# Attention on one core: the scores, too, in 2x2 blocks with Strassen's seven products

## Chip, cores, metric

One core of one Trainium2 chip. The metric is the device time of one execution in microseconds (us).

## The reference

Inputs q, k and v are float32, 8 x 2048 x 512. The result has the same shape.

```python
scores = np.matmul(q, k.transpose(0, 2, 1)) / np.sqrt(512)
attn_weights = special.softmax(scores, axis=-1).astype(np.float32)
return np.matmul(attn_weights, v)
```

## The kernel before

A query tile has 512 queries, so there are 32 tiles (4 in each of 8 batches). Scores are kept transposed: 128 keys on the partitions, 512 queries along the columns. Matmuls are in fp16 and sum in fp32 in tiles of PSUM; the kernel uses eight such tiles of 512 fp32 columns, called banks here. The output product (exponentials times v) is already computed in 2x2 blocks with the seven products of Strassen's method in Winograd's form; the scores are computed plainly. While the output products of tile g run, the scores of tile g + 1 are put between them.

```python
ps_st = ... tile_pool(name="ps_st", bufs=3, space=PSUM)    # scores
ps_x  = ... bufs=2;   ps_y = ... bufs=1;   ps_z = ... bufs=2   # outputs: 5 banks
# ... cut
def qk_tile(g, kb):                      # 128 keys x 512 queries
    # ... cut
    for dc in range(ND):                 # ND = 4
        nc.tensor.matmul(st[:], kT[b, c][:, n, dc, :], qT[b, qt][:, :, dc, :],
                         start=(dc == 0), stop=(dc == ND - 1))
    nc.scalar.activation(out=pt[:, kb // 2, kb % 2, :], in_=st[:], func=EXP, scale=inv_sqrt_d)

def p_sums(g, j0, j1):                   # sums of exponentials for the output products
    # ... cut
    nc.vector.tensor_add(s1[:, js], a21, a22)
    nc.vector.tensor_sub(a21, a11, a21)
    nc.vector.tensor_sub(s2[:, js], s1[:, js], a11)
    nc.vector.tensor_sub(s4[:, js], a12, s2[:, js])

class Pair:                              # two output blocks; pairs "a" and "b" in each tile
    def product(self, n):
        # ... cut: eight 128x256 matmuls into bank x, y or z
        getattr(self, f"after{n}", lambda: None)()
    def scaled(self, tag, src, r):       # VectorE
        t = small.tile([P, H], F32, tag=tag)
        nc.vector.tensor_scalar_mul(out=t[:], in0=src, scalar1=r[:])
        return t
    def after5(self):
        nc.vector.reciprocal(out=self.r2[:], in_=self.z[:, H:H + 1])   # r2: cut
        self.p5 = self.scaled("p5", self.z[:, 0:H], self.r2)
    # ... cut: after3, after2, after6, after7, after4

ORDER = "a1 a5 b5 a3 b1 a2 a6 b3 a7 b2 b6 a4 b7 b4".split()
# ... cut
p_sums(0, NJ - GROUP, NJ)                # end of the prologue
dma_transpose("q", 0, 1)                 # the second query tile
```

The softmax here doesn't subtract the row's maximum and nothing guards it: scores larger than these inputs give would overflow.

## Time and profile before

| | |
|---|---|
| time | 871.78 us (median of 3 runs, 871.65 to 871.78) |
| TensorE (PE) / VectorE (DVE) / ScalarE (ACT) busy | 97% / 55% / 35% |
| one score tile, one output product | 0.87 us each |

The first fence is from the page of the kernel before: its span, busy time by engine, granted clock in 40 slices, and the chain of waits that ended last by engine and by line.

```profile
span 870.3 us, 13872 instructions
...
PE 846.7 (97%) x5712; PEld 557.3 (64%) x5712; DVE 475.1 (55%) x1162; ACT 307.0 (35%) x513; POOL 72.7 (8%) x116
...
PEclk9799999999999999999999999999999999999999
...
PE 95%; DMA 4%; DVE 0%; issue 0%; POOL 0%; ACT 0%; POOLq 0%
```

After the prologue TensorE works almost without a pause, and the chain of waits stays on it. The next fence is the timeline of TensorE in the middle of the kernel before. The columns are start, length of the merged piece, engine, line, operation, and what is written from what. A piece's length (1.03 us) runs past the start of the next piece (0.87 us later), so rates are read from start to start.

```profile
453.13 1.03 PE L142 MATMUL st<-t 128*128 128x512 f16 x4
454.00 1.04 PE L193 MATMUL x<-t,pt 128*128 128x256 f16 x8
454.87 1.03 PE L142 MATMUL st<-t 128*128 128x512 f16 x4
```

Four matmuls of 512 columns take 0.87 us, and so do eight of 256 columns, each with its own weight load: 109 ns for one of 256. TensorE's waits in the whole execution (waits view: total us, times, longest) are few:

```profile
PE tr L100 <- DMA t<-in_q_dram: 9.5, 1, 9.5
PE st L142 <- DMA t<-t: 9.1, 1, 9.1
PE x L193 <- DVE o L206: 0.6, 1, 0.6
```

The first is the start. The second is in the prologue, where the second query tile waits for its DMA transpose.

### The profile page before, as it was taken

What the parts mean: (1) busy time and instruction counts of PE and PEld (TensorE: products, weight loads), DVE (VectorE), ACT (ScalarE), POOL (GpSimd) and SP (SyncE); (2) the same over time, 40 slices, a digit from 0 to 9 for tenths busy, and PEclk for the clock granted to TensorE, in tenths of its full rate; (3) what the DMA queues carried; (4) which work ended last, traced back from release to release, by engine and by line L of the source; (5) the groups of instructions that cost most, each with busy time, mean ns of one, the idle gap of its engine ahead of it and who ended that gap; (6) DMA issues with size and microseconds to landing.
All of it is one profiled execution on the core that took longest, in us unless ns stands there. A gap on an engine that the chain in (4) does not pass through costs nothing.

```text
span 870.3 us, 13872 instructions
## 1 busy us (share of the span) xinstructions
PE 846.7 (97%) x5712; PEld 557.3 (64%) x5712; DVE 475.1 (55%) x1162; ACT 307.0 (35%) x513; POOL 72.7 (8%) x116
## 2 busy tenths in 40 slices
PE   5599999999999999999999999999999999999997
PEld 3266666666666666666666666666666666666666
DVE  3554755556555574455654466555654557455554
ACT  2233333333333333333333333333333333333331
POOL 3111002010020100200002000110002010000000
PEclk9799999999999999999999999999999999999999
DMA  9999954986579954997439985298753988511101
GB/s 154 165 177 200 168 130 99 203 138 131 119 127 191 151 116 98 164 190 152 113 82 187 166 158 130 54 213 163 133 122 83 205 141 142 109 49 49 41 32 74
DMA packets 192046, 115.74 MB, mean 133 GB/s; under 512 B 126448, under 2 KB 175600, under 8 KB 191984
## 3 DMA queue, kind: packets, MB, share of 16 engines
q0 software_dynamic: 50688, 50.34, 38.3%
q1 hardware_dynamic: 141296, 64.54, 32.5%
q8 instruction: 44, 0.72, 0.3%
q14 instruction: 18, 0.15, 0.1%
HBM read 100.70 MB, written 33.55 MB: 154 GB/s over the span
## 4 chain that ended last, share of the span: by engine, by line
PE 95%; DMA 4%; DVE 0%; issue 0%; POOL 0%; ACT 0%; POOLq 0%
PE st L142 49%; PE x L193 26%; PE z L193 13%; PE y L193 6%; DMA t<-t 2%; DMA t<-in_q_dram 2%; PE tr L100 0%; POOL t L81 0%; ACT pt L146 0%; DVE o L206 0%; DVE t L202 0%; DVE o L239 0%; DVE s L155 0%; DVE pt L156 0%; DVE s L158 0%
## 5 line engine op out<-in xcount | busy, mean ns | idle before, releaser
L142 PE MATMUL st<-t 128*128 128x512 f16 x2048 | 514.9, 380 | 9.4 <-DMA t<-t 9.1
L146 ACT ACTIVATE pt<-st 128x512 f16<-128x512 f32 x512 | 305.7, 597 | 546.0 <-PE st L142 546.0
L142 PEld LDWEIGHTS <-t 128*128 128x128 f16 x2048 | 200.4, 98 | 159.1 <-DMA t<-t 9.6
L193 PEld LDWEIGHTS <-pt 128*128 128x128 f16 x2048 | 200.5, 98 | 81.5 <-issue 8.6
L193 PEld LDWEIGHTS <-s 128*128 128x128 f16 x1536 | 150.3, 98 | 58.2 <-issue 0.5
L193 PE MATMUL x<-vh,pt 128*128 128x256 f16 x1024 | 133.6, 274 | 0.0
L202 DVE TENSOR_SCALAR t<-x,r 128x256 f32<-128x256 f32 x128 | 61.9, 484 | 72.0 <-PE x L193 69.7
L155 DVE TENSOR_TENSOR s<-pt 128x512 f16<-128x512 f16 x128 | 53.5, 418 | 64.7 <-ACT pt L146 64.7
L193 PE MATMUL z<-vh,s 128*128 128x257 f16 x512 | 66.7, 273 | 0.4 <-DVE t L202 0.4
L193 PE MATMUL x<-t,pt 128*128 128x256 f16 x512 | 66.2, 272 | 0.6 <-DVE o L206 0.6
L193 PE MATMUL z<-t,s 128*128 128x257 f16 x512 | 66.6, 273 | 0.0
L193 PE MATMUL y<-vh,pt 128*128 128x256 f16 x512 | 66.4, 273 | 0.0
L193 PE MATMUL x<-t,s 128*128 128x256 f16 x512 | 66.4, 273 | 0.0
L239 DVE TENSOR_SCALAR o<-x,r 128x256 f32<-128x256 f32 x64 | 30.9, 483 | 58.7 <-PE x L193 58.7
L206 DVE SCALAR_TENSOR_TENSOR o<-y,r,t 128x256 f32<-128x256 f32 x64 | 30.9, 484 | 57.8 <-PE y L193 57.8
L156 DVE TENSOR_TENSOR pt<-pt 128x512 f16<-128x512 f16 x128 | 54.4, 425 | 4.4
L158 DVE TENSOR_TENSOR s<-pt,s 128x512 f16<-128x512 f16 x128 | 54.4, 425 | 4.4
L157 DVE TENSOR_TENSOR s<-s,pt 128x512 f16<-128x512 f16 x128 | 53.4, 417 | 0.0
L217 DVE RECIPROCAL r<-z 128x1 f32<-128x1 f32 x64 | 10.7, 167 | 67.3 <-PE z L193 67.3
L81 POOL DMA_DIRECT2D t<-in_k_dram x32 | 24.5, 767 | 200.7 <-DMA t<-t 192.6
L81 POOL DMA_DIRECT2D t<-in_q_dram x32 | 24.5, 766 | 188.6 <-DMA t<-t 134.5
L222 DVE RECIPROCAL r<-z 128x1 f32<-128x1 f32 x64 | 10.6, 165 | 43.6 <-PE z L193 43.6
(18 smaller groups left out, 183.6 us busy)
## 6 DMA issues: line engine op xcount, KB each, us to landing
out_dram<-o SPq DMA_DIRECT2D x128, 256.0 KB, 2.5
t<-in_k_dram POOLq DMA_DIRECT2D x32, 512.0 KB, 10.4
t<-in_q_dram POOLq DMA_DIRECT2D x32, 512.0 KB, 8.9
vh<-in_v_dram POOLq DMA_DIRECT2D x32, 512.0 KB, 10.9
t<-t SPq DMA_TRANSPOSE x59, 4.9
ident<-attn_identity SPq DMA_DIRECT2D x1, 32.0 KB, 1.6
```

What stands on the lines that cost most here:

```text
L81: nc.gpsimd.dma_start(out=t[:], in_=srcs[what][b, :, c * CH:(c + 1) * CH, :])
L142: nc.tensor.matmul(st[:], kT[b, c][:, n, dc, :], qT[b, qt][:, :, dc, :], start=(dc == 0), stop=(dc == ND - 1),)
L146: nc.scalar.activation(out=pt[:, kb // 2, kb % 2, :], in_=st[:], func=EXP, scale=inv_sqrt_d)
L155: nc.vector.tensor_add(s1[:, js], a21, a22)
L156: nc.vector.tensor_sub(a21, a11, a21)
L157: nc.vector.tensor_sub(s2[:, js], s1[:, js], a11)
L158: nc.vector.tensor_sub(s4[:, js], a12, s2[:, js])
L193: nc.tensor.matmul(dst[:, 0:width], lhs(j), rhs(j), start=(first and j == 0), stop=(j == NJ - 1), skip_group_check=True,)
L202: nc.vector.tensor_scalar_mul(out=t[:], in0=src, scalar1=r[:])
L206: nc.vector.scalar_tensor_tensor(out=out_, in0=src, scalar=r[:], in1=other[:], op0=MULT, op1=ADD)
L217: nc.vector.reciprocal(out=self.r2[:], in_=self.z[:, H:H + 1])
L239: nc.vector.tensor_scalar_mul(out=self.o2[:, 0:H], in0=self.x[:, 0:H], scalar1=self.r2[:])
```

## The change

Scores are computed for groups of 256 + 256 keys and 512 queries in 2x2 blocks with seven products instead of eight. That is worth one eighth of the score columns on TensorE. It costs additions: four VectorE operations for each block of keys and of queries, and seven reads of PSUM per group by ScalarE and VectorE in place of four (the exponentials of four key blocks). So the output scalings move from VectorE to ScalarE. Scores now take four banks (two x, one y, one z) in place of three, and the outputs four in place of five, eight in all as before: the outputs' z has one buffer instead of two, and the order of the output products is rearranged. The first sum of a group belongs both to x and to y; ScalarE copies it into y's bank, and product 2 accumulates on it. In the prologue the second query tile is transposed on TensorE and its scores are computed plainly as well.

```diff
+    for name, bufs in (("qx", 2), ("qy", 1), ("qz", 1), ("px", 2), ("py", 1), ("pz", 1)):
@@ the sums for four key blocks (q_sums: four as well for a query tile; value sums as before, in four pieces per batch instead of two)
+    def k_sums(b, c):
+        nc.vector.tensor_add(s1[:], a21, a22)
+        nc.vector.tensor_sub(a21, a11, a21)
+        nc.vector.tensor_sub(s2[:], s1[:], a11)
+        nc.vector.tensor_sub(s4[:], a12, s2[:])
@@ one group: products 1, 5, 6, 3, 2 in its own period, 7 and 4 in the next
+        def after1(self):
+            self.y = bank("qy")
+            nc.scalar.copy(out=self.y[:], in_=self.x[:])
+        def after5(self):
+            nc.scalar.copy(out=self.cz[:, :, 1, :], in_=self.two(self.z))
+        def after6(self):
+            nc.scalar.copy(out=self.cz[:, :, 0, :], in_=self.two(self.x))
+        def after7(self):
+            nc.vector.tensor_add(self.cz[:, :, 1, :], self.two(self.x), self.cz[:, :, 1, :])
+        def after3(self):
+            nc.vector.tensor_add(self.cz[:, :, 0, :], self.two(self.z), self.cz[:, :, 0, :])
+        def after4(self):
+            exp(self.pt[:, self.js, 1, 0:QH], self.two(self.x))
+        def after2(self):
+            exp(self.pt[:, self.js, 0, 0:QH], self.two(self.y))
+        def exp_right(self):
+            exp(self.pt[:, self.js, :, QH:QTW], self.cz[:])          # 1024 columns
@@ output scalings
-            nc.vector.tensor_scalar_mul(out=t[:], in0=src, scalar1=r[:])
+            nc.scalar.activation(out=out_, in_=src, func=COPY, scale=r[:])
-    ORDER = "a1 a5 b5 a3 b1 a2 a6 b3 a7 b2 b6 a4 b7 b4".split()
+    ORDER = "a1 b1 a5 a3 a2 a6 a7 b5 a4 b3 b2 b6 b7 b4".split()
+    QORDER = ((0, 1), (1, 7), (0, 5), (0, 6), (1, 4), (0, 3), (0, 2))   # 1: of the group before
@@ 28 score slots per tile, an output product after every second one
+            add(qt, 21, "qsum", "q", 3)              # in every tile
+        # vsum at slots 14, 25 (first and second tile of a batch)
+        # ksum at slots 6, 26 (third tile) and 4, 11 (fourth)
+                    if at == 2:
+                        prev.exp_right()
+                    if at == 4:
+                        p_sums(prev.g, prev.n, 0)    # three sums
+                    if at == 5:
+                        p_sums(prev.g, prev.n, 1)    # the fourth
```

Below, S1 to S7 are the score products (four matmuls each), A1 to A7 and B1 to B7 the output products of the two pairs (eight each). Four groups of seven score products make a tile of 28 slots.

More of the change, by code (lines that the diff above doesn't have):

```diff
@@ L48 @@
     inv_sqrt_d = float(1.0 / np.sqrt(D))
+    G = 2
+    NG = NJ // G
+    COPY = mybir.ActivationFunctionType.Copy
     const = ctx.enter_context(tc.tile_pool(name="const", bufs=1))
-    stage = ctx.enter_context(tc.tile_pool(name="stage", bufs=4))
-    qkt = ctx.enter_context(tc.tile_pool(name="qkt", bufs=6))
+    stage = ctx.enter_context(tc.tile_pool(name="stage", bufs=3))
+    kpool = ctx.enter_context(tc.tile_pool(name="kpool", bufs=5))
+    qpool = ctx.enter_context(tc.tile_pool(name="qpool", bufs=3))
     vpool = ctx.enter_context(tc.tile_pool(name="vpool", bufs=2))
@@ L56, with bank @@
     small = ctx.enter_context(tc.tile_pool(name="small", bufs=2))
-    ps_st = ctx.enter_context(tc.tile_pool(name="ps_st", bufs=3, space=bass.MemoryType.PSUM))
-    ps_x = ctx.enter_context(tc.tile_pool(name="ps_x", bufs=2, space=bass.MemoryType.PSUM))
-    ps_y = ctx.enter_context(tc.tile_pool(name="ps_y", bufs=1, space=bass.MemoryType.PSUM))
-    ps_z = ctx.enter_context(tc.tile_pool(name="ps_z", bufs=2, space=bass.MemoryType.PSUM))
+    czpool = ctx.enter_context(tc.tile_pool(name="czpool", bufs=2))
+    psum = {}
+    for name, bufs in (("qx", 2), ("qy", 1), ("qz", 1), ("px", 2), ("py", 1), ("pz", 1)):
+        psum[name] = ctx.enter_context(
+            tc.tile_pool(name="ps_" + name, bufs=bufs, space=bass.MemoryType.PSUM)
+        )
+    def bank(name):
+        t = psum[name].tile([P, 512], F32, tag=name)
+        return t
     ctx.enter_context(tc.manual_schedule())
@@ L82, in load, with operands @@
         staged[what, b, c] = t
+    def operands(what):
+        pool = kpool if what == "k" else qpool
+        raw = pool.tile([P, CH, ND, P], F16, tag=what + "raw")
+        sums = [pool.tile([P, 2, 2, P], F16, tag=what + f"s{n}", name=what + f"s{n}") for n in (1, 2, 4)]
+        return [raw] + sums
     def dma_transpose(what, b, c):
         src = staged.pop((what, b, c))
-        t = qkt.tile([P, CH, ND, P], F16, tag=what + "T")
+        t = operands(what)
         nc.sync.dma_start_transpose(
-            out=t[:].rearrange("p n c r -> p (n c) r"),
+            out=t[0][:].rearrange("p n c r -> p (n c) r"),
             in_=src[:].rearrange("p n d -> p (n d)"),
@@ L94, in pe_transpose @@
         src = staged.pop((what, b, c))
-        t = qkt.tile([P, CH, ND, P], F16, tag=what + "T")
+        t = operands(what)
         for n in range(0, CH, 2):
-            tr = ps_st.tile([P, 2, ND, P], F16, tag="st")
+            tr = psum["px"].tile([P, 2, ND, P], F16, tag="px", name="tr")
             for m in range(2):
@@ L102, in pe_transpose, with k_blocks, q_blocks, q_sums @@
                     )
-            nc.vector.tensor_copy(out=t[:, n:n + 2], in_=tr[:])
+            nc.vector.tensor_copy(out=t[0][:, n:n + 2], in_=tr[:])
         (kT if what == "k" else qT)[b, c] = t
-    def load_v(b):
+    def k_blocks(t):
+        w = t[0][:].rearrange("p (j s) c r -> p j s c r", s=2)
+        return w[:, :, 0, 0:2], w[:, :, 0, 2:4], w[:, :, 1, 0:2], w[:, :, 1, 2:4]
+    def q_blocks(t):
+        w = t[0]
+        return w[:, 0:2, 0:2], w[:, 2:4, 0:2], w[:, 0:2, 2:4], w[:, 2:4, 2:4]
+    def k_sums(b, c):
+        t = kT[b, c]
+        a11, a12, a21, a22 = k_blocks(t)
+        _, s1, s2, s4 = t
+        nc.vector.tensor_add(s1[:], a21, a22)
+        nc.vector.tensor_sub(a21, a11, a21)
+        nc.vector.tensor_sub(s2[:], s1[:], a11)
+        nc.vector.tensor_sub(s4[:], a12, s2[:])
+    def q_sums(b, c):
+        t = qT[b, c]
+        b11, b12, b21, b22 = q_blocks(t)
+        _, t1, t2, t4 = t
+        nc.vector.tensor_sub(t1[:], b12, b11)
+        nc.vector.tensor_sub(b12, b22, b12)
+        nc.vector.tensor_sub(t2[:], b22, t1[:])
+        nc.vector.tensor_sub(t4[:], b21, t2[:])
+    def new_v(b):
         vh = vpool.tile([P, NJ, 2, VP], F16, tag="vh")
@@ L112, in load_v, with v_sums @@
         nc.gpsimd.memset(t1[:, :, H:H + 1], 1.0)
-        dst = vh[:].rearrange("p j s d -> p (j s) d")
-        for n in range(0, NKB, CH):
-            nc.gpsimd.dma_start(
-                out=dst[:, n:n + CH, 0:D], in_=srcs["v"][b, :, n:n + CH, :]
-            )
-        vs[b] = (vh, t1, t2, t4)
-    def v_sums(b, part):
+        vs[b] = (vh, t1, t2, t4)
+    def load_v(b, c):
+        dst = vs[b][0][:].rearrange("p j s d -> p (j s) d")
+        ns = slice(c * CH, (c + 1) * CH)
+        nc.gpsimd.dma_start(out=dst[:, ns, 0:D], in_=srcs["v"][b, :, ns, :])
+    def v_sums(b, c):
         vh, t1, t2, t4 = vs[b]
-        js = slice(part * NJ // 2, (part + 1) * NJ // 2)
+        js = slice(c * CH // 2, (c + 1) * CH // 2)
         b11, b12 = vh[:, js, 0, 0:H], vh[:, js, 0, H:D]
@@ L128, in v_sums, with new_p, exp, plain_tile @@
         nc.vector.tensor_sub(t4[:, js], b21, t2[:, js])
-    def qk_tile(g, kb):
+    def new_p(g):
+        pt = ppool.tile([P, NJ, 2, QTW], F16, tag="pt")
+        s1 = ppool.tile([P, NJ, QH], F16, tag="s1")
+        s2 = ppool.tile([P, NJ, QH], F16, tag="s2")
+        s4 = ppool.tile([P, NJ, QH], F16, tag="s4")
+        pts[g] = (pt, s1, s2, s4)
+    def exp(out_, in_):
+        nc.scalar.activation(out=out_, in_=in_, func=EXP, scale=inv_sqrt_d)
+    def plain_tile(g, kb):
         b, qt = divmod(g, NQT)
         if kb == 0:
-            pt = ppool.tile([P, NJ, 2, QTW], F16, tag="pt")
-            s1 = ppool.tile([P, NJ, QH], F16, tag="s1")
-            s2 = ppool.tile([P, NJ, QH], F16, tag="s2")
-            s4 = ppool.tile([P, NJ, QH], F16, tag="s4")
-            pts[g] = (pt, s1, s2, s4)
-        pt = pts[g][0]
-        st = ps_st.tile([P, QTW], F32, tag="st")
+            new_p(g)
+        st = bank("qz" if kb % 3 == 2 else "qx")
         c, n = divmod(kb, CH)
@@ L142, in qk_tile, with __init__, product, two @@
             nc.tensor.matmul(
-                st[:], kT[b, c][:, n, dc, :], qT[b, qt][:, :, dc, :],
+                st[:], kT[b, c][0][:, n, dc, :], qT[b, qt][0][:, :, dc, :],
                 start=(dc == 0), stop=(dc == ND - 1),
             )
-        nc.scalar.activation(
-            out=pt[:, kb // 2, kb % 2, :], in_=st[:], func=EXP, scale=inv_sqrt_d
-        )
-    def p_sums(g, j0, j1):
+        exp(pts[g][0][:, kb // 2, kb % 2, :], st[:])
+    class Group:
+        def __init__(self, g, n):
+            self.g, self.n = g, n
+            self.js = slice(n * G, (n + 1) * G)
+            b, qt = divmod(g, NQT)
+            self.a, self.b = kT[b, n], qT[b, qt]
+        def product(self, n):
+            a11, a12, a21, a22 = k_blocks(self.a)
+            b11, b12, b21, b22 = q_blocks(self.b)
+            _, s1, s2, s4 = self.a
+            _, t1, t2, t4 = self.b
+            if n == 1:
+                if self.n == 0:
+                    new_p(self.g)
+                self.pt = pts[self.g][0]
+                self.x = bank("qx")
+            elif n == 5:
+                self.z = bank("qz")
+            lhs, rhs, dst = {
+                1: (a11, b11, "x"),
+                2: (a12, b21, "y"),
+                3: (s4, b22, "z"),
+                4: (a22, t4, "x"),
+                5: (s1, t1, "z"),
+                6: (s2, t2, "x"),
+                7: (a21, b12, "x"),
+            }[n]
+            dst = getattr(self, dst)
+            for j in range(G):
+                for c in range(2):
+                    nc.tensor.matmul(
+                        dst[:, j * QH:(j + 1) * QH], lhs[:, j, c, :], rhs[:, :, c, :],
+                        start=(n in (1, 5) and j == 0 and c == 0), stop=(c == 1),
+                        skip_group_check=True,
+                    )
+            getattr(self, f"after{n}", lambda: None)()
+        def two(self, t):
+            return t[:].rearrange("p (j q) -> p j q", j=G)
+        def after1(self):
+            self.y = bank("qy")
+            nc.scalar.copy(out=self.y[:], in_=self.x[:])
+        def after5(self):
+            self.cz = czpool.tile([P, G, 2, QH], F32, tag="cz")
+            nc.scalar.copy(out=self.cz[:, :, 1, :], in_=self.two(self.z))
[11 more added lines that the diff above has]
+            exp(self.pt[:, self.js, :, QH:QTW], self.cz[:])
@@ L151, in p_sums @@
+    def p_sums(g, n, part=None):
         pt, s1, s2, s4 = pts[g]
-        js = slice(j0, j1)
+        js = slice(n * G, (n + 1) * G)
         a11, a21 = pt[:, js, 0, 0:QH], pt[:, js, 0, QH:QTW]
         a12, a22 = pt[:, js, 1, 0:QH], pt[:, js, 1, QH:QTW]
-        nc.vector.tensor_add(s1[:, js], a21, a22)
-        nc.vector.tensor_sub(a21, a11, a21)
-        nc.vector.tensor_sub(s2[:, js], s1[:, js], a11)
-        nc.vector.tensor_sub(s4[:, js], a12, s2[:, js])
+        if part in (None, 0):
+            nc.vector.tensor_add(s1[:, js], a21, a22)
+            nc.vector.tensor_sub(s2[:, js], s1[:, js], a11)
+            nc.vector.tensor_sub(a21, a11, a21)
+        if part in (None, 1):
+            nc.vector.tensor_sub(s4[:, js], a12, s2[:, js])
@@ L173, in product @@
             if n == 1:
-                self.x = ps_x.tile([P, 512], F32, tag="x")
+                self.x = bank("px")
             elif n == 2:
-                self.y = ps_y.tile([P, 512], F32, tag="y")
+                self.y = bank("py")
             elif n == 5:
-                self.z = ps_z.tile([P, 512], F32, tag="z")
+                self.z = bank("pz")
             lhs, rhs, dst = {
@@ L198, in product, with scaled, final @@
             getattr(self, f"after{n}", lambda: None)()
-        def scaled(self, tag, src, r):
-            t = small.tile([P, H], F32, tag=tag)
-            nc.vector.tensor_scalar_mul(out=t[:], in0=src, scalar1=r[:])
-            return t
-        def final(self, out_, src, r, other):
+        def scaled(self, out_, src, r):
+            nc.scalar.activation(out=out_, in_=src, func=COPY, scale=r[:])
+        def final(self, out_, src, r):
             nc.vector.scalar_tensor_tensor(
-                out=out_, in0=src, scalar=r[:], in1=other[:], op0=MULT, op1=ADD
+                out=out_, in0=src, scalar=r[:], in1=out_, op0=MULT, op1=ADD
             )
@@ L215, in after5 @@
         def after5(self):
+            self.o2 = opool.tile([P, D], F32, tag="o")
             self.r2 = small.tile([P, 1], F32, tag="r2")
             nc.vector.reciprocal(out=self.r2[:], in_=self.z[:, H:H + 1])
-            self.p5 = self.scaled("p5", self.z[:, 0:H], self.r2)
+            self.scaled(self.o2[:, H:D], self.z[:, 0:H], self.r2)
         def after3(self):
+            self.o1 = opool.tile([P, D], F32, tag="o")
             self.r1 = small.tile([P, 1], F32, tag="r1")
             nc.vector.reciprocal(out=self.r1[:], in_=self.z[:, H:H + 1])
-            self.c1 = self.scaled("c1", self.x[:, 0:H], self.r1)
@@ L224, in after3 @@
-            self.o1 = opool.tile([P, D], F32, tag="o")
+            self.scaled(self.o1[:, 0:H], self.x[:, 0:H], self.r1)
         def after2(self):
-            self.final(self.o1[:, 0:H], self.y[:, 0:H], self.r1, self.c1)
+            self.final(self.o1[:, 0:H], self.y[:, 0:H], self.r1)
         def after6(self):
-            u2 = self.scaled("u2", self.x[:, 0:H], self.r1)
-            self.final(self.o1[:, H:D], self.z[:, 0:H], self.r1, u2)
+            self.scaled(self.o1[:, H:D], self.x[:, 0:H], self.r1)
@@ L232, in after6 @@
+            self.final(self.o1[:, H:D], self.z[:, 0:H], self.r1)
             self.store(self.o1, 0)
         def after7(self):
-            self.o2 = opool.tile([P, D], F32, tag="o")
-            self.final(self.o2[:, H:D], self.x[:, 0:H], self.r2, self.p5)
+            self.final(self.o2[:, H:D], self.x[:, 0:H], self.r2)
         def after4(self):
-            nc.vector.tensor_scalar_mul(
-                out=self.o2[:, 0:H], in0=self.x[:, 0:H], scalar1=self.r2[:]
-            )
+            self.scaled(self.o2[:, 0:H], self.x[:, 0:H], self.r2)
@@ L242, in after4, with plan, add @@
             self.store(self.o2, 1)
-    ORDER = "a1 a5 b5 a3 b1 a2 a6 b3 a7 b2 b6 a4 b7 b4".split()
-    GROUP = 2
+    ORDER = "a1 b1 a5 a3 a2 a6 a7 b5 a4 b3 b2 b6 b7 b4".split()
+    QORDER = ((0, 1), (1, 7), (0, 5), (0, 6), (1, 4), (0, 3), (0, 2))
+    NS = len(QORDER) * NG
+    def plan():
+        at = {}
+        def add(qt, slot, *what):
+            at.setdefault((qt, slot), []).append(what)
+        for qt in range(NQT):
+            add(qt, 0, "load", "q", 3)
+            add(qt, 9, "trans", "q", 3)
+            add(qt, 21, "qsum", "q", 3)
+        add(0, 1, "newv")
+        for c, (lq, ls, sq, ss) in enumerate(((0, 1, 0, 14), (0, 5, 0, 25), (1, 1, 1, 14), (1, 5, 1, 25))):
+            add(lq, ls, "load", "v", c)
+            add(sq, ss, "vsum", "v", c)
+        add(1, 15, "load", "k", 0)
+        add(1, 25, "trans", "k", 0)
+        add(2, 6, "ksum", "k", 0)
+        add(2, 3, "load", "k", 1)
+        add(2, 13, "trans", "k", 1)
+        add(2, 26, "ksum", "k", 1)
+        add(2, 11, "load", "k", 2)
+        add(2, 20, "trans", "k", 2)
+        add(3, 4, "ksum", "k", 2)
+        add(2, 18, "load", "k", 3)
+        add(2, 27, "trans", "k", 3)
+        add(3, 11, "ksum", "k", 3)
+        return at
@@ L247, in prefetch @@
+    PLAN = plan()
     def prefetch(g, slot):
         b, qt = divmod(g, NQT)
-        b += 1
-        if b >= B:
-            return
-        if qt == 0:
-            if slot == 0:
-                load_v(b)
-                load("k", b, 0)
-                load("q", b, 0)
-                load("k", b, 1)
-                load("q", b, 1)
-        if qt == 1:
-            todo = {1: ("k", 0), 5: ("q", 0), 9: ("k", 1), 13: ("q", 1)}
-            if slot in todo:
-                dma_transpose(todo[slot][0], b, todo[slot][1])
-            if slot == 14:
-                load("k", b, 2)
-                load("k", b, 3)
-                load("q", b, 2)
-                load("q", b, 3)
@@ L269, in prefetch @@
-        if qt == 2:
-            if slot == 2:
-                v_sums(b, 0)
-            if slot == 6:
-                v_sums(b, 1)
-            todo = {6: ("k", 2), 11: ("k", 3), 15: ("q", 2)}
-            if slot in todo:
-                dma_transpose(todo[slot][0], b, todo[slot][1])
-        if qt == 3:
-            if slot == 4:
-                dma_transpose("q", b, 3)
+        todo = PLAN.get((qt, slot), [])
+        if g == 1:
+            todo = [x for x in PLAN.get((0, slot), ()) if x[0] == "newv" or x[1] == "v"] + todo
@@ new lines, in prefetch @@
+        for what in todo:
+            if what[0] != "newv" and what[1] == "q":
+                n = g + 2
+                if n >= B * NQT or n < NQT:
+                    continue
+                bb, c = divmod(n, NQT)
+            else:
+                bb = b + 1
+                if bb >= B:
+                    continue
+                c = what[2] if len(what) > 2 else 0
+            if what[0] == "newv":
+                new_v(bb)
+            elif what[0] == "load":
+                load_v(bb, c) if what[1] == "v" else load(what[1], bb, c)
+            elif what[0] == "trans":
+                dma_transpose(what[1], bb, c)
+            elif what[0] == "ksum":
+                k_sums(bb, c)
+            elif what[0] == "qsum":
+                q_sums(bb, c)
+            elif what[0] == "vsum":
+                v_sums(bb, c)
@@ L282 @@
+    NP = B * NQT
+    load("q", 0, 0)
     load("k", 0, 0)
-    load("q", 0, 0)
     load("k", 0, 1)
-    load("k", 0, 2)
+    dummy = bank("qy")
     pe_transpose("q", 0, 0)
     pe_transpose("k", 0, 0)
+    load("k", 0, 2)
     load("k", 0, 3)
+    new_v(0)
+    nc.tensor.matmul(dummy[:], ident[:], kT[0, 0][0][:, 0], start=True, stop=True)
     load("q", 0, 1)
-    load_v(0)
-    NG = B * NQT
     for kb in range(NKB):
-        qk_tile(0, kb)
+        plain_tile(0, kb)
         if kb % CH == 1 and kb // CH + 1 < NCH:
@@ L295 @@
             pe_transpose("k", 0, kb // CH + 1)
-            if kb // CH == 0:
-                load("q", 0, 2)
-            if kb // CH == 1:
-                load("q", 0, 3)
-        if kb % (2 * GROUP) == 0 and kb:
-            p_sums(0, kb // 2 - GROUP, kb // 2)
-    p_sums(0, NJ - GROUP, NJ)
-    dma_transpose("q", 0, 1)
-    dma_transpose("q", 0, 2)
-    dma_transpose("q", 0, 3)
-    v_sums(0, 0)
-    v_sums(0, 1)
-    for g in range(NG):
-        pair = {"a": Pair(g, 0), "b": Pair(g, 1)}
-        for slot in range(NKB):
-            prefetch(g, slot)
-            if g + 1 < NG:
-                qk_tile(g + 1, slot)
-                if slot % (2 * GROUP) == 0 and slot:
-                    p_sums(g + 1, slot // 2 - GROUP, slot // 2)
-            if slot < len(ORDER):
-                pair[ORDER[slot][0]].product(int(ORDER[slot][1]))
-        if g + 1 < NG:
-            p_sums(g + 1, NJ - GROUP, NJ)
+        if kb % (2 * G) == 0 and kb:
+            p_sums(0, kb // (2 * G) - 1)
@@ new lines, with pv @@
+        if kb == 3:
+            load_v(0, 0)
+        if kb == 7:
+            load_v(0, 1)
+        if kb == 11:
+            load_v(0, 2)
+            load_v(0, 3)
+            load("q", 0, 2)
+            load("q", 0, 3)
+    pe_transpose("q", 0, 1)
+    p_sums(0, NG - 1)
+    pairs = (Pair(0, 0), Pair(0, 1))
+    def pv(g, n):
+        pairs[ORDER[n][0] == "b"].product(int(ORDER[n][1]))
+    for kb in range(NKB):
+        plain_tile(1, kb)
+        if kb == 3:
+            dma_transpose("q", 0, 2)
+        if kb == 4:
+            dma_transpose("q", 0, 3)
+        if 6 <= kb < 14 and kb % 2 == 0:
+            v_sums(0, (kb - 6) // 2)
+        if kb % (2 * G) == 0 and kb:
+            p_sums(1, kb // (2 * G) - 1)
+        if kb >= 14:
+            pv(0, kb - 14)
@@ new lines @@
+    p_sums(1, NG - 1)
+    for n in range(2, len(ORDER)):
+        pv(0, n)
+        if n < 6:
+            k_sums(0, n - 2)
+        if n == 6:
+            q_sums(0, 2)
+        if n == 7:
+            q_sums(0, 3)
+    prev = None
+    for g in range(1, NP):
+        pairs = (Pair(g, 0), Pair(g, 1))
+        for slot in range(NS):
+            if g + 1 < NP:
+                n, at = divmod(slot, len(QORDER))
+                if at == 0:
+                    cur = Group(g + 1, n)
+                old, what = QORDER[at]
+                if old == 0:
+                    cur.product(what)
+                elif prev is not None:
+                    prev.product(what)
+            elif slot in (1, 4):
+                prev.product(QORDER[slot][1])
+            if g + 1 < NP or slot < 7:
+                at = slot % len(QORDER)
+                if prev is not None:
+                    if at == 2:
[4 more added lines that the diff above has]
+                        p_sums(prev.g, prev.n, 1)
+                if at == len(QORDER) - 1 and g + 1 < NP:
+                    prev = cur
+            if slot % 2 == 1:
+                pv(g, slot // 2)
+            prefetch(g, slot)
```

## The prediction

> **What bounds the kernel now.** TensorE: by the page, PE is 97% busy (846.7 of 870.3 us), VectorE 55%, ScalarE 35%; the chain of waits is 95% PE, 49% on the score matmuls. By start-to-start times in the timeline, a score tile (four 128x512 matmuls) takes 0.865 us and a product of eight 128x256 matmuls with eight weight loads 0.873 us, 109 ns per matmul. One query tile is 16 x 0.865 + 14 x 0.873 = 26.1 us. The waits view shows one real PE gap: 9.1 us in the prologue, where the second query tile waits for its DMA transpose, with a slower clock after it (0.66, then 0.93 in the windows view).
>
> **What the change does, per query tile (30 of 32).**
> - PE: 64 matmuls of 512 columns become 4 groups x 7 products x 4 = 112 of 256: 112 x 109 ns = 12.2 us in place of 13.85. Saves 1.6 us, all on the critical path: 30 x 1.6 = 48 us. Weight loads (98 ns) still fit under a 109 ns matmul, as in the last tile's outputs.
> - Prologue: the second tile's query block is transposed on PE and its scores run at once: the gap and the cold clock go, about -10 us net.
> - ScalarE: gains three 512-column copies per group (0.6 us each, from the 597 ns exponential) and eight 256-column scalings per tile, and one 1024-column exponential per group from SBUF in place of two. [...] Sum about 20 us per 24.4 us tile: 80%.
> - VectorE: loses eight 484 ns scalings per tile (-3.9 us); gains eight fp32 adds out of PSUM of 512 columns [...], and key and query sums (3.4 us). Sum about 21 us of 24.4: 85%.
>
> **Critical path.** Zero stalls would give 871.8 - 48 - 10 = about 812. But both helpers become 80 to 85% busy in strict order, and the score products hold four banks: one for z, one for y, two for x. Stepping through one period (7 score products, 3.5 output products, 6.1 us) with these durations, most handovers have 0.5 to 2 us of slack; the tight ones are x (the exponential after product 4, behind the 1024-column one, against the next group's product 1) and z (VectorE's add after product 3, behind the sums, against the next product 5). I allow 0.4 us of stall per tile, 12 us, and 2 us where tile 0's outputs meet the first key sums.
>
> **Predicted: 826 us, range 813 to 846.** Faster by over 2%: 0.90; within 2%: 0.08; slower: 0.02.
>
> **Right if:** the score products show about 3,360 matmuls of 256 columns at 109 ns start to start; one tile takes 24.5 to 25 us; the prologue gap is gone; VectorE 75 to 85% busy, ScalarE 70 to 82%; PE still over 95% of the chain; PE's waits on ScalarE and VectorE total 5 to 25 us in pieces under 1 us.
>
> **Wrong if:** ScalarE's copies into PSUM or pointer-scaled activations cost far more than estimated, or VectorE's adds exceed 0.9 us, so that a helper bounds the period (over 845); handovers stall at each group; or query loads with three staging buffers come too late for their transposes. If nothing stalls, 808 to 815. [...]

The changed kernel's trace has 475 ns for a scaling and 682 to 687 ns for an addition, so eight of each per tile take 3.8 and 5.5 us. The 826 us are the 812 us without stalls and the 14 us allowed for stalls, and that allowance was the author's estimate. "In strict order" is seen in the changed kernel's trace below: a scaling whose input was complete did not start while the exponential ahead of it waited (1.29 us).

## The result

| | median, us | lowest to highest | runs |
|---|---|---|---|
| before | 871.78 | 871.65 to 872.91 | 4 |
| changed | 954.82 | 950.79 to 958.30 | 4 |

The ratio is 1.095, with a 95% interval of 1.090 to 1.100. Here and below a ratio is the mean time of one kernel's fast runs over that of the other's of the same rounds, so it is not quite the ratio of the medians. The kernel became 9.5% slower; 826 us had been predicted, and at most 846.

These are the lines of the changed kernel's page that answer to those above:

```profile
span 954.6 us, 18101 instructions
...
PE 843.9 (88%) x7169; PEld 709.0 (74%) x7169; DVE 593.1 (62%) x1460; ACT 569.2 (60%) x1009; POOL 72.8 (8%) x116
...
PEclk9999989999998999999999999999999999999999
...
PE 40%; DVE 25%; ACT 15%; DMA 14%; issue 5%; POOL 0%; ACTq 0%; DVEq 0%; POOLq 0%
```

No engine is busy all the time: TensorE 88%, VectorE 62%, ScalarE 60%. The chain of waits now goes back and forth between three engines. That is the look of handovers that come late, not of an engine that has too much to do. TensorE's waits say who is late:

```profile
PE t L319 <- ACT o L327: 54.1, 66, 2.1
PE t L237 <- DVE cz L260: 29.1, 29, 2.6
PE t L237 <- ACT pt L188: 7.7, 20, 0.4
...
PE t L319 <- DVE o L330: 2.9, 4, 0.9
```

L319 are the output matmuls, L237 the score matmuls; L327 is ScalarE's output scaling, L260 VectorE's addition after S7. The groups of the changed kernel show what the operations cost that the change added or moved. The columns are engine, operation, names, form and count, then total busy us and mean ns of one, then idle time before it and its releaser:

```profile
L327 ACT ACTIVATE o<-t,r 128x256 f32<-128x256 f32 x256 | 121.5, 475 | 180.9 <-DVE r L342 107.9
...
L188 ACT ACTIVATE pt<-cz 128x1024 f16<-128x1024 f32 x120 | 127.4, 1061 | 47.4 <-DVE cz L260 47.4
...
L237 PE MATMUL t<-qs,raw 128*128 128x256 f16 x480 | 72.3, 273 | 29.1 <-DVE cz L260 29.1
L260 DVE TENSOR_TENSOR cz<-t,cz 128x512 f32<-128x512 f32 x120 | 82.4, 687 | 24.3 <-PE t L237 24.1
...
L250 ACT COPY t<-t 128x512 f32<-128x512 f32 x120 | 68.4, 570 | 23.9 <-PE t L237 21.5
```

None was dear: the scaling took 475 ns (484 on VectorE in the kernel before), the addition 687 (the prediction's limit was 0.9 us), the seed copy 570 (estimated 600). The 1024-column exponential and S4 (`qs,raw`) both wait for the addition at L260. The timeline shows how this comes about, in a tile in which no DMA is late (all engines, lines left out):

```profile
438.95 0.60 PE L237 MATMUL t<-raw 128*128 128x256 f16 x4
...
439.61 0.42 DVE L151 TENSOR_TENSOR qs<-raw 128x512 f16<-128x512 f16 x1
...
439.83 1.04 PE L319 MATMUL t<-t,s 128*128 128x256 f16 x8
...
440.06 0.42 DVE L152 TENSOR_TENSOR raw<-raw 128x512 f16<-128x512 f16 x1
440.40 0.42 DVE L153 TENSOR_TENSOR qs<-raw,qs 128x512 f16<-128x512 f16 x1
...
440.86 0.42 DVE L154 TENSOR_TENSOR qs<-raw,qs 128x512 f16<-128x512 f16 x1
...
441.20 0.68 DVE L260 TENSOR_TENSOR cz<-t,cz 128x512 f32<-128x512 f32 x1
441.92 1.06 ACT L188 ACTIVATE pt<-cz 128x1024 f16<-128x1024 f32 x1 [1.29 <-DVE cz L260]
441.94 0.60 PE L237 MATMUL t<-qs,raw 128*128 128x256 f16 x4 [0.64 <-DVE cz L260]
...
442.88 0.46 ACT L327 ACTIVATE o<-t,r 128x256 f32<-128x256 f32 x1
...
443.39 1.03 PE L319 MATMUL t<-vh,pt 128*128 128x256 f16 x8 [0.85 <-ACT o L327]
```

S7, the first line, has ended by 439.6. Its addition, L260, stands in VectorE's queue behind the four query sums (L151 to L154), which nobody needs before the next tile, and starts at 441.2. Its reader S4 waits 0.64 us. But ScalarE has waited as well, 1.29 us, with the exponential at the head of its queue; behind that stands a scaling (L327) whose input, the sum of B6 (439.83 to 440.87), was complete two microseconds before it started, and for that scaling B7 (the last line) waits another 0.85 us. One block of sums in the wrong place has stopped TensorE twice, by way of two queues.

ScalarE started nothing behind the exponential in those 1.29 us, although the scaling's input was complete for the last 1.05 us of them.

Every matmul is in this trace, so each stall can be laid to a product: the time by which a product's first matmul starts later than 109 ns after the matmul before it. From the first group of the main loop to the last matmul, 885.3 us pass. Of these 121.7 us are such stalls, 18.9 us are extra time within products (a slow clock, see the end), and 744.6 us remain as work. The stalls are almost all at five places:

| stall before | S4 | A3 | B7 | S1 | B4 | others | sum |
|---|---|---|---|---|---|---|---|
| us in all | 34.0 | 30.5 | 29.9 | 11.0 | 7.7 | 8.6 | 121.7 |

### The profile page after: what moved, and what is told of

Read it like the earlier page. It is cut to its first block, busy times and chain, and to the rows that moved or that the text cites. A ratio compares the mean times of both kernels' runs of the same rounds, so it can differ in the third digit from the quotient of the medians.

```text
span 954.6 us, 18101 instructions
## 1 busy us (share of the span) xinstructions
PE 843.9 (88%) x7169; PEld 709.0 (74%) x7169; DVE 593.1 (62%) x1460; ACT 569.2 (60%) x1009; POOL 72.8 (8%) x116
## 3 DMA queue, kind: packets, MB, share of 16 engines
q1 hardware_dynamic: 139216, 64.01, 31.2%
## 4 chain that ended last, share of the span: by engine, by line
PE 40%; DVE 25%; ACT 15%; DMA 14%; issue 5%; POOL 0%; ACTq 0%; DVEq 0%; POOLq 0%
PE t L319 20%; PE t L237 16%; DMA raw<-t 14%; ACT pt L188 7%; ACT o L327 5%; DVE o L330 4%; PE t L198 3%; DVE cz L260 3%; DVE cz L263 3%; ACT cz L254 2%; DVE s L280 2%; DVE pt L282 1%; DVE s L284 1%; DVE raw L152 1%; DVE qs L154 1%
## 5 line engine op out<-in xcount | busy, mean ns | idle before, releaser
L319 PEld LDWEIGHTS <-pt 128*128 128x128 f16 x2048 | 204.8, 100 | 69.8 <-issue 41.8
L237 PEld LDWEIGHTS <-raw 128*128 128x128 f16 x1920 | 189.8, 99 | 69.2 <-issue 45.3
L319 PE MATMUL t<-vh,pt 128*128 128x256 f16 x1536 | 207.1, 280 | 26.3 <-ACT o L327 26.3
L327 ACT ACTIVATE o<-t,r 128x256 f32<-128x256 f32 x256 | 121.5, 475 | 180.9 <-DVE r L342 107.9
L188 ACT ACTIVATE pt<-t 128x512 f16<-128x512 f32 x272 | 163.7, 602 | 83.9 <-PE t L237 57.4
L237 PE MATMUL t<-raw 128*128 128x256 f16 x1440 | 204.1, 276 | 7.7 <-ACT pt L188 7.7
L319 PEld LDWEIGHTS <-s 128*128 128x128 f16 x1536 | 150.5, 98 | 53.5 <-issue 33.4
L330 DVE SCALAR_TENSOR_TENSOR o<-t,r,o 128x256 f32<-128x256 f32 x192 | 92.5, 482 | 114.0 <-ACT o L327 81.2
L237 PEld LDWEIGHTS <-ks 128*128 128x128 f16 x1440 | 143.8, 100 | 23.6 <-issue 1.8
L188 ACT ACTIVATE pt<-cz 128x1024 f16<-128x1024 f32 x120 | 127.4, 1061 | 47.4 <-DVE cz L260 47.4
L237 PE MATMUL t<-qs,ks 128*128 128x256 f16 x960 | 137.2, 277 | 1.0 <-DVE cz L263 1.0
L280 DVE TENSOR_TENSOR s<-pt 128x512 f16<-128x512 f16 x128 | 54.1, 422 | 129.7 <-ACT pt L188 129.7
L319 PE MATMUL t<-t,s 128*128 128x257 f16 (+1 forms) x1024 | 133.1, 273 | 0.8 <-DVE o L330 0.8
L237 PE MATMUL t<-qs,raw 128*128 128x256 f16 x480 | 72.3, 273 | 29.1 <-DVE cz L260 29.1
L260 DVE TENSOR_TENSOR cz<-t,cz 128x512 f32<-128x512 f32 x120 | 82.4, 687 | 24.3 <-PE t L237 24.1
L254 ACT COPY cz<-t 128x512 f32<-128x512 f32 x120 | 70.2, 585 | 43.3 <-PE t L237 39.2
L319 PE MATMUL t<-vh,s 128*128 128x257 f16 x512 | 68.4, 277 | 27.8 <-ACT o L327 27.8
L263 DVE TENSOR_TENSOR cz<-t,cz 128x512 f32<-128x512 f32 x120 | 81.9, 682 | 5.6 <-PE t L237 5.6
L237 PE MATMUL t<-raw,ks 128*128 128x256 f16 x480 | 75.4, 281 | 0.5 <-ACT cz L254 0.5
L319 PE MATMUL t<-t,pt 128*128 128x256 f16 x512 | 68.2, 277 | 5.0 <-DVE o L330 2.1
L257 ACT COPY cz<-t 128x512 f32<-128x512 f32 x120 | 69.6, 580 | 1.9 <-PE t L237 1.8
```

The lines of the kernel that those rows point to most:

```text
L188: nc.scalar.activation(out=out_, in_=in_, func=EXP, scale=inv_sqrt_d)
L237: nc.tensor.matmul(dst[:, j * QH:(j + 1) * QH], lhs[:, j, c, :], rhs[:, :, c, :], start=(n in (1, 5) and j == 0 and c == 0), stop=(c == 1) ...
L254: nc.scalar.copy(out=self.cz[:, :, 1, :], in_=self.two(self.z))
L257: nc.scalar.copy(out=self.cz[:, :, 0, :], in_=self.two(self.x))
L260: nc.vector.tensor_add(self.cz[:, :, 1, :], self.two(self.x), self.cz[:, :, 1, :])
L263: nc.vector.tensor_add(self.cz[:, :, 0, :], self.two(self.z), self.cz[:, :, 0, :])
```

## The experiments

The theories were these. **A**: blocks of four sums (1.7 us) stand in VectorE's queue ahead of an operation for which TensorE waits. **A2**, for the rest: output products stand one slot behind a product whose sum must be read first. **B**: ScalarE and VectorE are short of throughput. **C**: late DMA transposes hold up the sums (VectorE waited 9.2 us for them in all, by the waits view; the 14% of DMA in the chain of waits is far more, because the chain counts a transpose from its issue on: in one place of q_22, 21.6 us for a wait of 0.9). **D**: moving the scalings to ScalarE is the fault by itself.

In some expectations below, "stepping through the queues" is a schedule worked out on paper: it lets each engine take its operations in program order, with the durations of the changed kernel's trace. It gave 28.5 us for a tile of the changed kernel, where the trace has 29.0 on average.

All kernels tried gave correct results. The kernel before was run again in every round, with medians of 871.63 to 872.10 us, so times of different rounds are compared directly. The stalls by the account used above, in us (S1 to S7, A and B as there):

| kernel | S4 | A3 | B7 | S1 | B4 | others | all stalls | slow clock within products |
|---|---|---|---|---|---|---|---|---|
| changed | 34.0 | 30.5 | 29.9 | 11.0 | 7.7 | 8.6 | 121.7 | 18.9 |
| q_22 | 1.2 | 30.6 | 13.6 | 10.9 | 14.7 | 7.0 | 78.0 | 8.0 |
| sums_moved | 0.0 | 19.5 | 13.6 | 0.0 | 9.7 | 1.6 | 44.4 | 1.4 |
| scal_dve | 34.8 | 31.2 | 0.9 | 0.2 | 15.2 | 6.0 | 88.3 | 11.7 |
| order_only | 0.0 | 19.4 | 0.7 | 0.0 | 0.0 | 5.5 | 25.6 | 1.4 |
| spaced | 0.0 | 9.5 | 0.7 | 0.0 | 0.0 | 5.4 | 15.6 | 1.4 |
| spaced_q21 | 45.4 | 9.6 | 0.7 | 0.0 | 0.1 | 5.5 | 61.3 | 2.8 |

### q_22: the query sums one slot later

```diff
-            add(qt, 21, "qsum", "q", 3)
+            add(qt, 22, "qsum", "q", 3)
```

> Only the place of the four query sums of each tile in VectorE's queue changes: one slot later (22 in place of 21), so behind the add of product 7 of the same group instead of ahead of it. Theory A (blocks of four sums issued ahead of an operation that TensorE waits for): the stall before product 4 in slot 25 (34 us in all in the changed kernel) and half of the one before product 7 of the second pair (30 us) go; stepping through the queues with durations of the trace gives 1.2 us per tile, so about 915 us. Theory B (ScalarE and VectorE short of throughput): the work is the same, so no change, 955 us. Theory C (late DMA transposes hold the sums): 0.4 us more slack only, at most 10 us, 945 us or more.

Measured: 901.30 us (898.81 to 903.28, 4 runs), ratio to before 1.034. One number in the schedule took 54 us off. TensorE's waits of q_22:

```profile
PE t L319 <- ACT o L327: 39.1, 66, 2.1
PE t L319 <- DVE o L330: 8.7, 10, 1.1
...
PE t L237 <- DVE cz L260: 0.9, 1, 0.9
```

The wait for L260 fell from 29.1 to 0.9 us, and that for ScalarE's scaling from 54.1 to 39.1 us. The same sums now stand behind the addition, and S4 goes through. Theories B and C, which foresaw 945 us or more, do not explain this. Not all of it went: B4's stall rose from 7.7 to 14.7 us. The trace shows where: in six tiles, each the first of a batch, it is 1.0 to 1.2 us, where the changed kernel has 0.0 to 0.1. In these six the sums waited 0.8 to 1.0 us for their DMA transpose, and in the one looked at closely they and the sums of the exponentials behind them hold up the addition (L330) for which B4 waits. So theory C has a part of some 6 us here; that is a reading of the traces, which no run isolated.

### sums_moved: all sums in idle slots

```diff
-            add(qt, 21, "qsum", "q", 3)
+            add(qt, 26, "qsum", "q", 3)
@@ value sums of the four chunks, (tile of the batch, slot)
-        (0, 14), (0, 25), (1, 14), (1, 25)
+        (0, 17), (1, 8), (1, 17), (2, 2)
@@ key sums of chunks 1 to 3 (chunk 0 stays at (2, 6))
-        (2, 26), (3, 4), (3, 11)
+        (3, 1), (3, 8), (3, 16)
```

> All key, query and value sums are issued in slots where VectorE was idle in the trace or where nobody waits for what follows; their number, sizes and operands are the same. Theory A: 2.4 us of the 4.1 us of stall per tile go (73 us), and the slow-clock time that follows stalls mostly with them (up to 20 us): 860 to 880 us, about level with the kernel before. Left are about 1.5 us per tile: product 3 of the first pair right after 5, product 7 after 6 and 4 after 7 of the second. Theory B: no change, 955 us. Theory C: only what the late transposes cost, 9 us of waiting by the waits view and what it delays, 930 us or more.

Measured: 862.30 us (860.18 to 865.71, 4 runs), ratio 0.990 (0.987 to 0.992). The same instructions in another place take 92 us less. The page and TensorE's waits of sums_moved:

```profile
span 859.9 us, 18121 instructions
...
PE 813.3 (95%) x7169; PEld 698.8 (81%) x7169; DVE 591.0 (69%) x1460; ACT 566.9 (66%) x1009; POOL 72.8 (8%) x116
```

```profile
PE t L319 <- ACT o L327: 27.0, 66, 1.1
...
PE t L319 <- DVE o L330: 2.9, 4, 0.9
```

VectorE is busy for 591 us as against 593 us before the move: its work did not change. Theory A holds, and B and C fall as main causes. The slow-clock time went with the stalls (18.9 to 1.4 us).

### scal_dve: the output scalings back on VectorE

```diff
-            nc.scalar.activation(out=out_, in_=src, func=COPY, scale=r[:])
+            nc.vector.tensor_scalar_mul(out=out_, in0=src, scalar1=r[:])
```

> The eight output scalings per tile go back from ScalarE to VectorE (0.48 us each), all else as in the changed kernel. Theory B (throughput): VectorE's busy time rises from 593 to about 715 us and it becomes the bound, so slower than 955 us. Theory D (ScalarE's queue: scalings stuck behind the 1024-column exponential are the main cost): the stall before product 7 of the second pair (30 us) goes and with it up to half of the rest. Theory A: the stalls behind the sums stay (products 4 and 3), only the one in ScalarE's queue goes: stepping through the queues gives 1.3 us per tile less, about 915 us.

Measured: 912.08 us (909.46 to 917.15, 4 runs), ratio 1.045. This is faster than the changed kernel although VectorE's busy time rose to 707 us, so B falls once more. TensorE's waits of scal_dve:

```profile
PE t L319 <- DVE o L327: 32.2, 36, 2.9
PE t L237 <- DVE cz L260: 29.8, 29, 3.0
```

The wait behind the sums is untouched (29.8 us). What went is B7's stall (29.9 to 0.9 us), which came from ScalarE's queue, and S1's (11.0 to 0.2); B4's rose (7.7 to 15.2). By this run alone, D could be taken as half right; spaced_sdve below decides it.

### before_q1: the prologue's part alone, on the kernel before

```diff
-    dma_transpose("q", 0, 1)
+    pe_transpose("q", 0, 1)
```

> The kernel before, with only the second query block of the prologue transposed on TensorE instead of by DMA. If the 9.1 us gap of the prologue is what that part of the change takes away, and the slow clock after it (about 2 us): 861 us, 10 to 11 us under the kernel before.

Measured: 867.02 us (866.21 to 867.32, 4 runs), ratio 0.9945. That is 4.6 us under the kernel before in the same rounds (871.63), half of what was expected. The timeline of the prologue of before_q1:

```profile
30.22 1.06 PE L100 MATMUL tr<-ident,t 128*128 128x128 f16 x16
...
31.05 0.42 DVE L155 TENSOR_TENSOR s<-pt 128x512 f16<-128x512 f16 x1 [1.77 <-ACT pt L146]
...
32.65 1.28 DVE L103 COPY t<-tr 128x1024 f16<-128x1024 f16 x2
...
33.99 1.89 PE L142 MATMUL st<-t 128*128 128x512 f16 x4 [2.71 <-DVE t L103]
```

It is the same fault on a small scale. The last sums of exponentials (L155 and on) stand in VectorE's queue ahead of the copy of the transposes, and TensorE still waits 2.71 us. In the changed kernel the transposes stand ahead of those sums, and this wait is 0.9 us.

### order_only: sums_moved with another order of the output products

```diff
-    ORDER = "a1 b1 a5 a3 a2 a6 a7 b5 a4 b3 b2 b6 b7 b4".split()
+    ORDER = "a1 b1 a5 a3 a2 a6 a7 b5 b3 b2 b6 b7 a4 b4".split()
```

> On top of the moved sums only the order of the output products changes: product 4 of the first pair goes from behind product 5 of the second to between 7 and 4 of the second. Claim under test: what is left of the stalls is products that follow, one output slot later (0.87 us of score work), a product whose sum ScalarE or VectorE must first read. In the trace of the moved sums, 7 after 6 and 4 after 7 of the second pair cost 0.44 and 0.31 us per tile, and 3 after 5 of the first 0.63 us. The second of them should go wholly (0.31), the first mostly, since the one read by VectorE comes sooner; 3 after 5 stays: 25.8 us per tile becomes 25.0 to 25.2, 862 becomes 838 to 848 us. Rival (ScalarE or VectorE short of throughput): order does not matter, 862 us.

Measured: 845.09 us (844.48 to 845.78, 4 runs), ratio 0.969. The stalls before B7 and B4, 23.3 us together in sums_moved, are 0.7 us now. A3's is unchanged, as expected. This is theory A2.

### spaced: the fourth sum of the exponentials one slot later

```diff
-                    if at == 5:
+                    if at == 6:
                         p_sums(prev.g, prev.n, 1)
```

> As the kernel with the new order, and the fourth sum of the exponentials is issued one slot later, so that the reciprocal for product 5 of the first pair no longer stands behind it in VectorE's queue. Estimate: 3 after 5 of the first pair falls from 0.63 to about 0.25 us per tile; 24.7 to 24.9 us per tile, 828 to 838 us, 0.4 us per tile under the order alone. Rival: no difference to the order alone.

Measured: 834.53 us (834.13 to 835.26, 4 runs), ratio 0.957 (0.956 to 0.958). A3's stall halved (19.4 to 9.5 us); all tiles but the first take 24.8 us. The page of spaced:

```profile
PE 805.0 (97%) x7169; PEld 699.3 (84%) x7169; DVE 594.7 (71%) x1460; ACT 573.3 (69%) x1009; POOL 72.8 (9%) x116
...
PE 79%; ACT 7%; DVE 6%; DMA 5%; issue 2%; POOL 0%; DVEq 0%; POOLq 0%; ACTq 0%
```

Compared with the changed kernel, spaced issues the same 7169 matmuls, 1460 VectorE and 1009 ScalarE instructions. It runs 120 us faster and stands 4.3% under the kernel before.

### spaced_q21: the control

```diff
-            add(qt, 26, "qsum", "q", 3)
+            add(qt, 21, "qsum", "q", 3)
```

> Control, the other way round: spaced with nothing but the four query sums put back ahead of the add of product 7 (slot 21). Theory A: product 4 of that group waits 1.3 to 1.5 us again in every tile, 30 x 1.4 = 42 us over spaced, about 870 to 880 us. If the place of the sums in the queue were not the cause, the same as spaced.

Measured: 881.3 us, a single run of unknown state, so its profile counts for more than its time. TensorE's waits of spaced_q21:

```profile
PE t L237 <- DVE cz L260: 40.8, 28, 3.0
PE t L319 <- ACT o L327: 8.0, 8, 3.1
```

Only S4's stall came back, 45.4 us in all; in spaced it was nil. It was 1.3 to 1.4 us in most tiles, and 2.5 to 3.2 us in six, each the first of a batch, where the sums also waited 0.9 to 1.6 us for their transpose. So theory C has a part in it: about 1.5 us in each of the six, 9 us in all. That is a reading of this trace; no run isolated it.

### spaced_pro: tile 0's outputs among the second tile's scores

```diff
-        if 6 <= kb < 14 and kb % 2 == 0:
-            v_sums(0, (kb - 6) // 2)
+        if kb in (1, 2, 3, 5):
+            v_sums(0, (1, 2, 3, 5).index(kb))
-        if kb >= 14:
-            pv(0, kb - 14)
+        if kb >= 6:
+            pv(0, kb - 6)
+        # key sums at kb 6, 9, 13; the rest among the outputs that are left
```

> As spaced, and tile 0's output products are spread over the second tile's scores (from its 7th score tile on) in place of standing alone with the key and query sums after it. In the trace of the moved sums those 12 products alone took 17.6 us, where 12 x 0.873 = 10.5 us of work; so 4 to 7 us less than spaced.

Measured: 832.01 us (827.92 to 835.82, 4 runs), ratio 0.954 (0.950 to 0.958). In the profiles the first score group starts at 61.1 us instead of 66.4. But the times scatter more, and the interval overlaps that of spaced: a gain of 2.5 us in the medians, which these runs do not settle.

### spaced_sdve: the scalings back on VectorE, in spaced

The edit is that of scal_dve.

> spaced, with the eight output scalings per tile back on VectorE, the same edit as in scal_dve. There it took 43 us off the changed kernel. If that had been because ScalarE is the wrong engine for them, it helps here too, below 834 us. If it helped only by getting them out of the queue behind the late 1024-column exponential, which in spaced is no longer late, then it only loads VectorE (about 710 us of busy time in 830, against 595): stepping through the queues gives 26.8 in place of 24.9 us per tile, so about 885 us, slower by some 50 us.

Measured: 869.64 us (869.39 to 870.23, 4 runs), ratio 0.998. The edit that took 43 us off the changed kernel adds 35 us here. VectorE is then busy for 703.7 us, 81% of the span, and TensorE's waits are mostly those of A2 again (by the account above A3 16.1, A7 14.1 and B7 9.6 us, of 49.8 in all):

```profile
PE t L319 <- DVE o L327: 34.4, 62, 2.9
```

So theory D falls: in spaced's order of work the scalings belong on ScalarE, and in the changed kernel their removal helped by taking them out of a queue that had been stopped.

## Why the prediction was wrong

Right were:

- **The work on TensorE.** The trace has 3360 score matmuls of 256 columns at 109 ns. The work left in the main loop is 744.6 us in the changed kernel and the same in spaced. With most stalls taken out, the predicted 826 us is nearly reached (834.5 and 832.0 us), and the predicted 24.5 to 25 us per tile is met (24.8); in the changed kernel itself a tile took 29.0.
- **The prologue gap.** It fell from 9.1 to 0.9 us. What that was worth in the changed kernel no run isolates; on the kernel before, the same edit brought 4.6 of the 10 us predicted.
- **The durations.** The seed copy took 570 ns, where 600 had been estimated, and the addition 682 to 687 ns, under the limit of 0.9 us. The scaling took 475 ns. The seeded sum gave correct results in every run; why it should was not shown by a trace.

Wrong was one step, the stalls: "I allow 0.4 us of stall per tile, 12 us, and 2 us where tile 0's outputs meet the first key sums." Measured were 121.7 us, 4.1 us per tile, and 18.9 us of slow clock that came with them; tile 0's outputs lost 7 us (17.6 us for 10.5 us of work, in the traces of the changed kernel and of sums_moved alike). The sum goes: 826 - 14 + 122 + 19 + 7 = 960 us, where 955 were measured. The runs show three things that this step left out:

1. **The sums were counted as load, not as blocks with a place.** The prediction enters them as 3.4 us of a tile's 21 and does not say where in the queue they stand. In the queue they are blocks of 1.7 us, and what counts is what stands right behind each. By q_22 and sums_moved their place was worth 54 and 92 us. Of the two tight handovers that the prediction named, z (seen as S5's stall) cost 1.6 us and x (S1's) 11.0; the costly one, the addition after S7, it had not seen.
2. **Only handovers of the score banks are named as tight.** The output products had lost z's second buffer and been given a new order, but none of their handovers appears in the prediction. A3 after A5 and B7 after B6 leave one slot, 0.87 us, for the end of the product, a reciprocal, a scaling and the queues before them; A3, B7 and B4 together cost 68 us. Of this, moving the sums took 25 us, and order_only and spaced took another 33.
3. **A late operation delays not only its reader but all that stands behind that reader.** The allowance of 0.4 us leaves no room for this. In the trace above B7 waited 0.85 us on a scaling that was ready, behind an exponential that waited 1.29 us for VectorE.

The busy shares, too, were foreseen too high: VectorE 75 to 85% and ScalarE 70 to 82%, against 62% and 60% measured (71% and 69% in spaced). The warning that "a helper bounds the period" was not what happened. Both had over a third of their time free and were late all the same.

## What to carry to other kernels

When work moves onto helper engines that take it in order, as ScalarE did in the 1.29 us above, do not stop at their busy shares: write down, for each handover that the bounding engine waits for, what stands ahead of it in the helper's queue, and what stands behind its reader. Put blocks of work that nobody needs soon behind the urgent operation, into a stretch where the queue would wait anyway; here one slot was worth 54 us of 955. If, as here, everything is busy 60 to 90% and the chain of waits wanders between engines, suspect order first, and try moving the same instructions before giving up the algorithm.

## What else the traces measured

- The slow clock. After the prologue TensorE had no idle gap longer than 2.65 us in the changed kernel, and the granted clock in its trace was halved 13 times before the end of the kernel, twelve times for 3.4 us and once for 6.8 us. 11 of the 13 began within 2.2 us after a wait of 1.6 to 2.65 us, and two more waits of that length (2.05 and 2.06 us) had no such effect. The cost is about the 18.9 us within products. Windows view of the changed kernel, three stretches in a row; the column before the last two is the granted clock:

```profile
405.00:411.00 6.00, 5.62 (x50) 4.68 (x48) 3.29 (x9) 4.37 (x9) 0.14 (x1) 1.00 1.09 199
411.00:412.60 1.60, 0.04 (x1) 0.00 (x0) 1.57 (x4) 0.00 (x0) 0.60 (x1) 1.00 0.60 109
412.60:418.50 5.90, 4.96 (x29) 3.67 (x29) 4.31 (x12) 2.99 (x5) 0.00 (x0) 0.71 0.67 134
```

- Order alone. Here it was worth 92 us of 955 with the same instructions (sums_moved), on engines that were 60% busy.
- Copies by ScalarE. A 512-column copy out of PSUM took 570 ns into PSUM and, by line and run, 573 to 585 ns into SBUF, so 3 to 15 ns more. The copies into SBUF also write two separate pieces of 256 columns; no run tells the two effects apart.
- Additions by VectorE. An fp32 addition of 512 columns with one operand in PSUM took 682 to 687 ns in the changed kernel.
